# A fixed TensorE order for the small products of a chunked RWKV-7 scan, and two of its products interleaved

## The chip, the cores and the metric

The kernel runs on one core of a Trainium2 chip (trn2). The metric is the time of one execution on the device, in microseconds, of which the median over several runs is given. The core's engines work side by side, each through its own list of instructions: TensorE (PE in the profile, with its weight loads shown apart as PEld), VectorE (DVE), ScalarE (ACT), GpSimd (POOL) and SyncE (SP, which issues most transfers). They meet at semaphores.

## The reference

A decoder block of width 1024 over 1024 tokens. One projection feeds two groups of heads: a spatial gating unit and an RWKV-7 recurrence with 8 heads of 64. Their outputs go through `w_out`, then comes a cross attention over 256 memory tokens and a last RMS norm. All of it is in float32. The change touches the recurrence only:

```python
def rwkv7_step(state, inp):
    r, w, k, v, a, bb = inp
    sa = jnp.einsum('bhvk,bhk->bhv', state, a)
    state = state * w[:, :, None, :] + sa[..., None] * bb[:, :, None, :] + v[..., None] * k[:, :, None, :]
    y = jnp.einsum('bhvk,bhk->bhv', state, r)
    return state, y
...
_, y = lax.scan(rwkv7_step, state0, (r, decay, k, v, -kk, kk * icl))
```

## The kernel before

The large projections run as triples of matmuls (`mm3`, lines 177 to 179): every operand is split into a high and a low part, and three products of 128 x 128 by 128 x 512 are summed. They are called dense steps below.

The recurrence is cut into chunks of 64 tokens. Work goes by halves of a head pair: 4 pairs of heads, 2 halves of 512 tokens, so 8 units `u` of 8 chunks, and a unit has two quarters of 4 chunks. The two heads of a pair (`hh`) lie on partitions 0 to 63 and 64 to 127 (`R[0]`, `R[1]`). A unit goes through these steps, all of them small float32 products:

- `grams(i)` (lines 639 to 684): for each quarter 16 products of 64 x 64 by 64 x 128 (line 655). A product reads head `hh` from one half of the partitions and writes to half `x`, so the 16 use all four 64 x 64 quarters of the array (row half `hh`, column half `x`). The results lie in two PSUM banks, one for each head. From them VectorE makes masked matrices, which go to DRAM (`nt_scr`) and come back as diagonal blocks of 16 x 16. VectorE inverts these in a loop (lines 672 to 678) and the result returns through DRAM (`t_img`) as `t16`, in four transfers (line 683).
- `turn(n)` (lines 687 to 704) transposes operands on TensorE.
- `solve(i)` (lines 706 to 751) builds the inverse of a 64 x 64 triangular matrix for each chunk and head out of `t16`. It is a chain of stages. Each is a `pair_mm` (lines 713 to 718): 16 products of 64 x 64 by 64 x 64, eight chunks by two heads, on two quarters of the array, rows and columns `R[hh]`. The four on the chain write to the bank `cb`; VectorE works on the result (lines 731, 734 and 735, 739, 743) before the next may start. The last two, `at` by `tt` to `cb` and `tt` by `akv` to `co`, have no VectorE step between them. ScalarE copies their results to `ra` (line 747) and, in four pieces, to `avt` (line 750).
- `serial(i)` (lines 753 to 790) carries the state over the chunks, with two products for each (lines 773 and 780) and VectorE between them.
- `outputs(n)` (lines 792 to 803): 8 products of 128 x 64 by 64 columns for each quarter (line 800). `finish(u)` follows.

`drive` (lines 897 to 922) puts these steps and the dense steps into one order, by estimated costs and due times. A second scheduler, the one of the language, then sets the order on each engine when the kernel is built, and it may move instructions past each other. So the order on TensorE isn't the one of the code. `cb_ps` has one buffer, `co_ps` two.

Of the kernel before, what the change touches and what calls it, by code (L numbers as in the profile page):

```python
# [18 lines left out]
P = 128  # L19
# [4 lines left out]
NC = HT // C  # L24
# [4 lines left out]
QC = 4  # L29
# [53 lines left out]
def tile_hybrid_block(ctx: ExitStack, tc: tile.TileContext, x, xT, mem, memT, cst_d, vec_d, w_sv, w_blk, w2_d, a2_d,  # L83
# [372 lines left out]
    with tc.tile_pool(name="rw", bufs=1) as rw:  # L456
# [182 lines left out]
        def grams(i):  # L639
# [6 lines left out]
            for j in range(2):  # L646
                gr = rw.tile([P, QC, 2, C], F32, name="gr", bufs=4)
                an = rw.tile([P, QC, C], F32, name="an", bufs=2)
                nt1 = rw.tile([P, QC, C], F32, name="nt1", bufs=2)
                ak1 = rw.tile([P, QC, C], F32, name="ak1", bufs=2)  # L650
                pss = [co_ps().rearrange("p (c x t) -> p c x t", c=QC, x=2) for _ in range(2)]
                for c in range(QC):
                    cc = QC * j + c
                    for hh, x in ((0, 0), (1, 1), (0, 1), (1, 0)):
                        nc.tensor.matmul(pss[hh][R[x], c, :, :], bk[R[hh], cc, x, :], ra[R[hh], cc, :, :],  # L655
                                         start=True, stop=True)
                for hh in (1, 0):
                    ps = pss[hh]
                    if hh == 0:
                        nc.vector.tensor_tensor(out=an, in0=ps[:, :, 1, :], in1=m_a, op=ALU.mult)  # L660
                    else:
                        nc.vector.tensor_tensor(out=nt1[64:128], in0=ps[0:64, :, 1, :], in1=m_a[0:64], op=ALU.mult)
                        nc.vector.tensor_tensor(out=ak1[64:128], in0=ps[64:128, :, 1, :], in1=m_a[64:128], op=ALU.mult)
                    nc.sync.dma_start(out=ns[j, hh, :, 0:C, :].rearrange("c s t -> s c t"), in_=(an, nt1)[hh][R[hh]])
                    nc.vector.tensor_tensor(out=gr[:, :, hh, :], in0=ps[:, :, 0, :], in1=m_r, op=ALU.mult)
                    yield
                quarters[2 * i + j].update(gr=gr, ntl=(an, nt1), akl=(an, ak1))
                if j == 0:

                    L, X = [flat(t)[0:64].rearrange("p (s t) -> p s t", s=16) for t in (ak1, nt1)]  # L670
# [16 lines left out]
        def turn(n):  # L687
# [15 lines left out]
            q.update(avt=avt, bkt=bkt)  # L703
            yield

        def solve(i):


# [3 lines left out]

            def pair_mm(ps, fl, fr):
                ps = ps.rearrange("p (c t) -> p c t", c=NC)
                for c in range(NC):
                    for hh in range(2):
                        nc.tensor.matmul(ps[R[hh], c, :], fl(hh, c), fr(hh, c), start=True, stop=True)  # L717
                return ps

            tt = rw.tile([P, NC, C], F32, name="tt")  # L720
# [21 lines left out]
            ps = pair_mm(cb_ps(), lambda hh, c: z2[R[hh], c, :], lambda hh, c: tt[R[hh], c, :])  # L742
            nc.vector.tensor_tensor(out=tt[:, :, 32:64], in0=tt[:, :, 32:64], in1=ps[:, :, 32:64], op=ALU.add)
            yield
            ps = pair_mm(cb_ps(), lambda hh, c: at[R[hh], c, :], lambda hh, c: tt[R[hh], c, :])
            pa = pair_mm(co_ps(), lambda hh, c: tt[R[hh], c, :], lambda hh, c: akv[R[hh], c, :])
            nc.scalar.copy(out=ra[:, :, 1, :], in_=ps)
            for j in range(2):
                for hh in range(2):
                    nc.scalar.copy(out=qs[j]["avt"][R[0], :, R[hh]], in_=pa[R[hh], QC * j:QC * j + QC, :])  # L750
            yield

        def serial(i):
# [38 lines left out]
        def outputs(n):  # L792
# [1 line left out]
            q, u = quarters[n], quarters[n]["u"]  # L794
            gr, avt = q["gr"], q["avt"]
            yps = psC.tile([P, 512], F32, name="yps")
            for c in range(QC):
                for hh in range(2):
                    o = P * (c // 2) + 64 * hh
                    nc.tensor.matmul(yps[R[c % 2], o:o + 64], gr[:, c, hh, :], avt[:, c, R[hh]], start=True, stop=True)  # L800
            yt = u["y"][:, 2 * (n % 2):2 * (n % 2) + 2, :]
            nc.vector.tensor_tensor(out=yt, in0=yt, in1=yps[:, 0:256].rearrange("p (c v) -> p c v", c=2), op=ALU.add)
            yield
# [400 lines left out]
```

## Time and profile before

| | |
|---|---|
| runs shown | 953.72, 956.23 and 956.41 us, median 956.23 us |
| the profiled execution | 960.05 us, its span 958.3 us |
| PE busy | 926.8 us, 97% of the span |
| DVE busy | 582.0 us, 61% |
| ACT busy | 396.3 us, 41% |
| mean granted TensorE clock | 0.990 |

The span runs from the first to the last instruction. The busy time of an engine is the union of its instructions; where matmuls overlap, it counts once. A float32 product is two records in the profile (two passes), one of a dense step is one.

### The profile page before, as it was taken

The page shows a single profiled execution, that of the slowest core. Times are in us where ns is not written, and L with a number is a line of the kernel's source. Part 1 is how long each engine was busy: PE and PEld are TensorE (multiplying, and loading weights), DVE is VectorE, ACT ScalarE, POOL GpSimd, SP SyncE. Part 2 cuts the span into 40 slices and gives each one's busy share as a digit, 9 for nine tenths or more (in the row PEclk, how much of TensorE's full clock was granted, in tenths as well). Part 3 has the DMA queues.
Part 4 walks back from the last instruction along what each step waited for, and adds up shares of the span by engine and source line. Part 5 has one row for each costly group of instructions (what it writes and reads, how often), then busy time and mean ns, then how long its engine had stood idle before and what let it go on. Part 6 is the DMA issues. An engine that isn't in the chain of part 4 may idle for free.

```text
span 958.3 us, 17336 instructions
## 1 busy us (share of the span) xinstructions
PE 926.8 (97%) x6876; PEld 747.4 (78%) x6876; DVE 582.0 (61%) x1307; ACT 396.3 (41%) x802; POOL 49.6 (5%) x113
## 2 busy tenths in 40 slices
PE   6999999999999999999999999999899999999997
PEld 6978888888777777777777776777698778888885
DVE  5867233344674958586858698787677664433333
ACT  6753222225352526162526372435256653333222
POOL 0001000011000000000000000000000000000000
PEclk9999999999999999999999999899999999999999
DMA  9762011223121111111111174324462400000011
GB/s 318 256 213 80 31 66 66 68 72 109 36 58 36 40 23 50 35 51 30 52 32 43 27 211 148 101 60 141 150 211 70 123 22 1 23 23 23 28 39 44
DMA packets 86096, 76.93 MB, mean 80 GB/s; under 512 B 38272, under 2 KB 58752, under 8 KB 86016
## 3 DMA queue, kind: packets, MB, share of 16 engines
q1 hardware_dynamic: 84864, 73.73, 25.3%
q10 hardware_dynamic: 1152, 2.10, 0.6%
q8 instruction: 54, 0.88, 0.4%
q14 instruction: 26, 0.21, 0.1%
HBM read 62.17 MB, written 13.64 MB: 79 GB/s over the span
## 4 chain that ended last, share of the span: by engine, by line
PE 80%; DVE 8%; DMA 5%; ACT 3%; issue 3%; POOL 1%; POOLq 0%; SPq 0%; ACTq 0%; DVEq 0%
PE mm L177 21%; PE mm L179 20%; PE mm L178 20%; PE cb L717 4%; PE co L655 3%; PE co L717 2%; PE us L773 2%; PE us L780 1%; DMA w_raw<-y_scr 1%; PE yps L800 1%; POOL grs L153 1%; DMA w_raw<-in_w_sv 1%; DMA p_raw<-in_w_kv 1%; PE co L634 1%; PE co L432 1%
## 5 line engine op out<-in xcount | busy, mean ns | idle before, releaser
L177 PE MATMUL mm<-xh,w_hi 128*128 128x512 f32 x400 | 166.1, 415 | 0.0
L178 PE MATMUL mm<-xl,w_hi 128*128 128x512 f32 x400 | 160.0, 400 | 0.0
L179 PE MATMUL mm<-xh,w_lo 128*128 128x512 f32 x400 | 159.4, 398 | 0.0
L157 DVE TENSOR_TENSOR w_lo<-w_raw,w_hi 128x512 fp32r<-128x512 f32 x115 | 78.6, 686 | 62.0 <-ACT w_hi L156 61.3
L156 ACT CAST w_hi<-w_raw 128x512 fp32r<-128x512 f32 x115 | 70.9, 617 | 103.7 <-PE mm L178 90.6
L179 PEld LDWEIGHTS mm<-xh,w_lo 128*128 128x128 f32 x400 | 75.2, 188 | 15.6 <-issue 0.9
L177 PEld LDWEIGHTS mm<-xh,w_hi 128*128 128x128 f32 x400 | 75.3, 188 | 15.3 <-issue 2.1
L178 PEld LDWEIGHTS mm<-xl,w_hi 128*128 128x128 f32 x400 | 75.4, 188 | 14.2 <-issue 1.3
L177 PE MATMUL mm<-wo,w_hi 128*128 128x512 f32 x128 | 53.9, 421 | 0.0
L179 PE MATMUL mm<-wo,w_lo 128*128 128x512 f32 x128 | 53.0, 414 | 0.0
L178 PE MATMUL mm<-wo,w_hi 128*128 128x512 f32 x128 | 52.4, 409 | 0.0
L177 PE MATMUL mm<-vp_h,p_hi 128*128 128x512 f32 x128 | 51.3, 401 | 0.0
L498 ACT ACTIVATE t<-mm,vec 128x512 f32<-128x512 f32 x34 | 23.3, 687 | 65.0 <-PE mm L179 52.8
L179 PE MATMUL mm<-kp_h,w_lo 128*128 128x512 f32 x128 | 50.1, 391 | 0.0
L177 PE MATMUL mm<-kp_h,w_hi 128*128 128x512 f32 x128 | 50.0, 391 | 0.0
L179 PE MATMUL mm<-vp_h,p_lo 128*128 128x512 f32 x128 | 50.0, 390 | 0.0
L178 PE MATMUL mm<-vp_l,p_hi 128*128 128x512 f32 x128 | 49.9, 390 | 0.0
L178 PE MATMUL mm<-kp_l,w_hi 128*128 128x512 f32 x128 | 49.9, 389 | 0.0
L1041 DVE TENSOR_REDUCE mx<-mm 128x2 f32<-128x512 f32 x16 | 11.1, 691 | 41.8 <-PE mm L179 41.8
L655 PE MATMUL co<-ra,bk 64*64 64x128 f32 x512 | 35.5, 282 | 0.5 <-ACT avt L750 0.2
L786 DVE SCALAR_TENSOR_TENSOR stdiag<-us,dc,sd 64x64 f32<-64x64 f32 x112 | 31.7, 283 | 4.4 <-PE us L780 0.7
L789 ACT COPY ytok<-us 64x128 f32<-64x128 f32 x60 | 15.4, 256 | 43.6 <-DVE stdiag L786 34.1
(276 smaller groups left out, 2035.9 us busy)
## 6 DMA issues: line engine op xcount, KB each, us to landing
w_raw<-in_w_blk SPq DMA_DIRECT2D x50, 256.0 KB, 2.8
w_raw<-y_scr SPq DMA_DIRECT2D x32, 256.0 KB, 3.6
w_raw<-in_w_kv SPq DMA_DIRECT2D x17, 256.0 KB, 3.9
xr<-in_xT SPq DMA_DIRECT2D x8, 512.0 KB, 5.3
w_raw<-in_w_out SPq DMA_DIRECT2D x16, 256.0 KB, 2.8
h_all<-in_x SPq DMA_DIRECT2D x16, 256.0 KB, 5.0
pr<-in_w_qT SPq DMA_DIRECT2D x8, 512.0 KB, 4.5
w_raw<-in_w_o SPq DMA_DIRECT2D x16, 256.0 KB, 2.7
```

The lines of the kernel that those rows point to most:

```text
L156: nc.scalar.copy(out=hi, in_=src)
L157: (eng or nc.vector).tensor_tensor(out=lo, in0=src, in1=hi.bitcast(F32), op=ALU.subtract)
L177: nc.tensor.matmul(ps, lh, rh, start=first, stop=False)
L178: nc.tensor.matmul(ps, lh, rl, start=False, stop=False)
L179: nc.tensor.matmul(ps, ll, rh, start=False, stop=last)
L498: nc.scalar.activation(out=t1[:, 1:HT + 1], in_=ps, func=AF.Copy, scale=vc("mu", b))
L655: nc.tensor.matmul(pss[hh][R[x], c, :, :], bk[R[hh], cc, x, :], ra[R[hh], cc, :, :], start=True, stop=True)
L717: nc.tensor.matmul(ps[R[hh], c, :], fl(hh, c), fr(hh, c), start=True, stop=True)
L773: nc.tensor.matmul(us[:, 0, :], ra[:, c, :, :], s_old, start=True, stop=True)
L786: nc.vector.scalar_tensor_tensor(out=s_new[h2, h2], in0=us[h2, 1, h2], scalar=dcc[h2], in1=sd[h2, h2], op0=ALU.mult, op1=ALU.add)
L789: nc.scalar.copy(out=yc, in_=us[R[0], 0, :])
L1041: nc.vector.tensor_reduce(out=m2, in_=ps.rearrange("p (h m) -> p h m", h=2), axis=AX.X, op=ALU.max)
```

## The change

Three places get a block `with together():`, in which TensorE keeps the order of the code: the 16 products of `grams` (line 655), every `pair_mm` and the 8 products of `outputs`. In `pair_mm` and `outputs` that order now runs from the last chunk to the first, and in `pair_mm` from head 1 to head 0. The last two stages of `solve` become one loop of 32 products. For each chunk there are two to `cb` on the quarters (row half, column half) = (0, 0) and (1, 1), as before, and two to `co` on (0, 1) and (1, 0): their results change halves, and the ScalarE copies read the other half.

```diff
--- before.py
+++ after.py
@@ -649,11 +649,11 @@
                 nt1 = rw.tile([P, QC, C], F32, name="nt1", bufs=2)
                 ak1 = rw.tile([P, QC, C], F32, name="ak1", bufs=2)
                 pss = [co_ps().rearrange("p (c x t) -> p c x t", c=QC, x=2) for _ in range(2)]
-                for c in range(QC):
-                    cc = QC * j + c
-                    for hh, x in ((0, 0), (1, 1), (0, 1), (1, 0)):
-                        nc.tensor.matmul(pss[hh][R[x], c, :, :], bk[R[hh], cc, x, :], ra[R[hh], cc, :, :],
-                                         start=True, stop=True)
+                with together():
+                    for c in range(QC * j, QC * j + QC):
+                        for hh, x in ((0, 0), (1, 1), (0, 1), (1, 0)):
+                            nc.tensor.matmul(pss[hh][R[x], c % QC, :, :], bk[R[hh], c, x, :], ra[R[hh], c, :, :],
+                                             start=True, stop=True)
                 for hh in (1, 0):
                     ps = pss[hh]
                     if hh == 0:
@@ -703,6 +703,10 @@
             q.update(avt=avt, bkt=bkt)
             yield
 
+        def together():
+
+            return tc.manual_schedule(engines={mybir.EngineType.PE})
+
         def solve(i):
 
 
@@ -712,9 +716,10 @@
 
             def pair_mm(ps, fl, fr):
                 ps = ps.rearrange("p (c t) -> p c t", c=NC)
-                for c in range(NC):
-                    for hh in range(2):
-                        nc.tensor.matmul(ps[R[hh], c, :], fl(hh, c), fr(hh, c), start=True, stop=True)
+                with together():
+                    for c in range(NC - 1, -1, -1):
+                        for hh in (1, 0):
+                            nc.tensor.matmul(ps[R[hh], c, :], fl(hh, c), fr(hh, c), start=True, stop=True)
                 return ps
 
             tt = rw.tile([P, NC, C], F32, name="tt")
@@ -742,12 +747,18 @@
             ps = pair_mm(cb_ps(), lambda hh, c: z2[R[hh], c, :], lambda hh, c: tt[R[hh], c, :])
             nc.vector.tensor_tensor(out=tt[:, :, 32:64], in0=tt[:, :, 32:64], in1=ps[:, :, 32:64], op=ALU.add)
             yield
-            ps = pair_mm(cb_ps(), lambda hh, c: at[R[hh], c, :], lambda hh, c: tt[R[hh], c, :])
-            pa = pair_mm(co_ps(), lambda hh, c: tt[R[hh], c, :], lambda hh, c: akv[R[hh], c, :])
+
+            ps, pa = [t.rearrange("p (c t) -> p c t", c=NC) for t in (cb_ps(), co_ps())]
+            with together():
+                for c in range(NC - 1, -1, -1):
+                    for r in R:
+                        nc.tensor.matmul(ps[r, c, :], at[r, c, :], tt[r, c, :], start=True, stop=True)
+                    for hh in range(2):
+                        nc.tensor.matmul(pa[R[1 - hh], c, :], tt[R[hh], c, :], akv[R[hh], c, :], start=True, stop=True)
             nc.scalar.copy(out=ra[:, :, 1, :], in_=ps)
             for j in range(2):
                 for hh in range(2):
-                    nc.scalar.copy(out=qs[j]["avt"][R[0], :, R[hh]], in_=pa[R[hh], QC * j:QC * j + QC, :])
+                    nc.scalar.copy(out=qs[j]["avt"][R[0], :, R[hh]], in_=pa[R[1 - hh], QC * j:QC * j + QC, :])
             yield
 
         def serial(i):
@@ -794,10 +805,12 @@
             q, u = quarters[n], quarters[n]["u"]
             gr, avt = q["gr"], q["avt"]
             yps = psC.tile([P, 512], F32, name="yps")
-            for c in range(QC):
-                for hh in range(2):
-                    o = P * (c // 2) + 64 * hh
-                    nc.tensor.matmul(yps[R[c % 2], o:o + 64], gr[:, c, hh, :], avt[:, c, R[hh]], start=True, stop=True)
+            with together():
+                for c in range(QC - 1, -1, -1):
+                    for hh in range(2):
+                        o = P * (c // 2) + 64 * hh
+                        nc.tensor.matmul(yps[R[c % 2], o:o + 64], gr[:, c, hh, :], avt[:, c, R[hh]],
+                                         start=True, stop=True)
             yt = u["y"][:, 2 * (n % 2):2 * (n % 2) + 2, :]
             nc.vector.tensor_tensor(out=yt, in0=yt, in1=yps[:, 0:256].rearrange("p (c v) -> p c v", c=2), op=ALU.add)
             yield
```

What it makes of TensorE's order is shown at three places. The first is the end of a solve and the grams behind it, in the fourth unit whose solve is followed by both. `tt,at` and `akv,tt` are the last two stages, `us` the state's products, `xh`, `xl` with `w_hi`, `w_lo` dense steps. Before:

```order
L717 MATMUL cb<-tt,at 64x64 x16
L717 MATMUL co<-akv,tt 64x64 x16
L773 MATMUL us<-stdiag_1924,ra 128x128
L655 MATMUL co<-ra,bk 64x128 x8
L780 MATMUL us<-avt,bkt 128x128
L655 MATMUL co<-ra,bk 64x128 x8
L179 MATMUL mm<-xh_99,w_lo 128x512
L773 MATMUL us<-stdiag_1925,ra 128x128
L655 MATMUL co<-ra,bk 64x128 x8
L177 MATMUL mm<-xh_100,w_hi 128x512
L655 MATMUL co<-ra,bk 64x128 x8
L780 MATMUL us<-avt,bkt 128x128
```

Now:

```order
L755 MATMUL cb<-tt,at 64x64 x2
L757 MATMUL co<-akv,tt 64x64 x2
L655 MATMUL co<-ra,bk 64x128
L179 MATMUL mm<-xh_100,w_lo 128x512
L177 MATMUL mm<-xh_101,w_hi 128x512
L784 MATMUL us<-stdiag_1924,ra 128x128
L178 MATMUL mm<-xl_109,w_hi 128x512
L179 MATMUL mm<-xh_101,w_lo 128x512
L177 MATMUL mm<-xh_102,w_hi 128x512
L791 MATMUL us<-avt,bkt 128x128
L655 MATMUL co<-ra,bk 64x128 x15
L784 MATMUL us<-stdiag_1925,ra 128x128
```

Before, the 16 products of a quarter stood in two groups of 8, one for each head, with other work between, and the two stages stood one behind the other. Now the 16 are 1 and 15 (so in all 16 quarters, and the one stands directly behind a solve's last product for 7 of them), and the two stages alternate by twos; the first seven such pairs of rows are left out ahead of the fence.

The second place is the solve's first stage of the same unit, which waits for `t16` (here `t_`, with `an` or `nt` as the other operand). Before, its second half:

```order
L177 MATMUL mm<-xh_102,w_hi 128x512
L717 MATMUL cb<-t_4122,an 64x64
L178 MATMUL mm<-xl_110,w_hi 128x512
L179 MATMUL mm<-xh_102,w_lo 128x512
L177 MATMUL mm<-xh_103,w_hi 128x512
L717 MATMUL cb<-t_4122,nt_4040 64x64
L717 MATMUL cb<-t_4122,an 64x64
L717 MATMUL cb<-t_4122,nt_4040 64x64
L717 MATMUL cb<-t_4122,an 64x64
L717 MATMUL cb<-t_4122,nt_4040 64x64
L717 MATMUL cb<-t_4122,an 64x64
L717 MATMUL cb<-t_4122,nt_4040 64x64
```

Now its end and what follows:

```order
L722 MATMUL cb<-t_4221,nt_4101 64x64
L722 MATMUL cb<-t_4221,an 64x64
L722 MATMUL cb<-t_4221,nt_4101 64x64
L722 MATMUL cb<-t_4221,an 64x64
L179 MATMUL mm<-xh_103,w_lo 128x512
L177 MATMUL mm<-xh_104,w_hi 128x512
L178 MATMUL mm<-xl_112,w_hi 128x512
L179 MATMUL mm<-xh_104,w_lo 128x512
L177 MATMUL mm<-xh_105,w_hi 128x512
L178 MATMUL mm<-xl_113,w_hi 128x512
L722 MATMUL cb<-zz_1926,tt 64x64 x16
```

Before, the 16 products stood as 1, 7, 1 and 7 with dense steps between, in each of the 8 solves. Now they follow each other without a break, the last chunk first.

The third place is the last solve of the program. Before, from the end of its third stage:

```order
L717 MATMUL cb<-t_6558,an 64x64
L717 MATMUL cb<-t_6558,nt_6481 64x64
L177 MATMUL mm<-wo,w_hi 128x512
L178 MATMUL mm<-wo,w_hi 128x512
L179 MATMUL mm<-wo,w_lo 128x512
L177 MATMUL mm<-wo,w_hi 128x512
L717 MATMUL cb<-tt,zz_1927 64x64 x16
L178 MATMUL mm<-wo,w_hi 128x512
L179 MATMUL mm<-wo,w_lo 128x512
L177 MATMUL mm<-wo,w_hi 128x512
L717 MATMUL cb<-tt,at 64x64 x16
L717 MATMUL co<-akv,tt 64x64 x16
```

Now, likewise:

```order
L722 MATMUL cb<-t_6789,nt_6674 64x64
L722 MATMUL cb<-t_6789,an 64x64
L722 MATMUL cb<-tt,zz_1927 64x64 x16
L755 MATMUL cb<-tt,at 64x64 x2
L757 MATMUL co<-akv,tt 64x64 x2
```

The dense steps between the stages are gone there: all four stages and the last 32 products stand in a row (64 and 32 products), behind 29 dense steps and four transposes that stand ahead of the first. In the other solves at least one dense step, mostly three, still stands between two stages.

Counted over the whole program, stretches in which TensorE leaves the full 128 x 128 array for quarters or halves of it and comes back were 131 and are now 112. No product is added or taken away.

## Rows read from the trace of the kernel before

**Rows 1.** The page's busy times: us, share of the span, instructions.

```profile
PE 926.8 (97%) x6876; PEld 747.4 (78%) x6876; DVE 582.0 (61%) x1307; ACT 396.3 (41%) x802; POOL 49.6 (5%) x113
```

**Rows 2.** The page's busy tenths in 40 slices, TensorE and its granted clock.

```profile
PE   6999999999999999999999999999899999999997
...
PEclk9999999999999999999999999899999999999999
```

**Rows 3.** The page's chain that ended last, by engine.

```profile
PE 80%; DVE 8%; DMA 5%; ACT 3%; issue 3%; POOL 1%; POOLq 0%; SPq 0%; ACTq 0%; DVEq 0%
```

**Rows 4.** Timeline of PE, a piece of 7 products: start, length, instruction, count.

```profile
486.46 0.40 PE L177 MATMUL mm<-xh,w_hi 128*128 128x512 f32 x1
486.79 0.27 PE L717 MATMUL cb<-t,nt 64*64 64x64 f32 x1
...
487.39 0.50 PE L178 MATMUL mm<-xl,w_hi 128*128 128x512 f32 x1
487.73 0.39 PE L179 MATMUL mm<-xh,w_lo 128*128 128x512 f32 x1
487.96 0.40 PE L177 MATMUL mm<-xh,w_hi 128*128 128x512 f32 x1
```

**Rows 5.** Timeline of PE, grams of one quarter in two halves.

```profile
351.24 1.09 PE L655 MATMUL co<-ra,bk 64*64 64x128 f32 x16
352.26 0.49 PE L780 MATMUL us<-avt,bkt 128*128 128x128 f32 x2
352.68 1.09 PE L655 MATMUL co<-ra,bk 64*64 64x128 f32 x16
353.70 0.50 PE L178 MATMUL mm<-xl,w_hi 128*128 128x512 f32 x1
```

**Rows 6.** Timeline of PE, the first unit's second quarter, in one piece.

```profile
263.16 1.33 PE L655 MATMUL co<-ra,bk 64*64 64x128 f32 x32
264.42 0.50 PE L177 MATMUL mm<-xh,w_hi 128*128 128x512 f32 x1
```

**Rows 7.** Timeline of PE, the last two stages of the last solve.

```profile
648.34 1.15 PE L717 MATMUL cb<-tt,at 64*64 64x64 f32 x32
649.32 1.10 PE L717 MATMUL co<-akv,tt 64*64 64x64 f32 x32
650.35 0.49 PE L773 MATMUL us<-stdiag,ra 128*128 128x128 f32 x2
```

**Rows 8.** PE's waits: us in total, times, longest.

```profile
PE us L773 <- ACT ytok L789: 1.8, 4, 0.6
PE cb L717 <- DVE t L734: 1.5, 2, 1.0
PE us L780 <- DVE avt L774: 1.2, 2, 0.7
...
PE cb L717 <- DMA t<-t_img: 0.5, 1, 0.5
```

**Rows 9.** Timelines of PE and SP: a unit's last half of grams, and its `t16` transfers.

```profile
501.77 1.09 PE L655 MATMUL co<-ra,bk 64*64 64x128 f32 x16
...
530.46 2.57 SPq L683 DMA_DIRECT2D t<-t_img  x4
...
606.79 1.97 PE L655 MATMUL co<-ra,bk 64*64 64x128 f32 x16
...
633.17 3.27 SPq L683 DMA_DIRECT2D t<-t_img  x4
```

**Rows 10.** The tile `t`: the time from issue to landing of its transfers.

```profile
DMA to landing us min/median/max: 2.3/2.5/4.1
```

**Rows 11.** Timelines of DVE and ACT in the last solve: start, length, instruction, count, idle time.

```profile
647.55 0.42 DVE L743 TENSOR_TENSOR tt<-tt,cb 128x256 f32<-128x256 f32 x1 [0.86 <-PE cb L717]
...
649.53 0.58 ACT L747 COPY ra<-cb 128x512 f32<-128x512 f32 x1 [4.50 <-PE cb L717]
650.47 1.52 ACT L750 COPY avt<-co 64x256 f32<-64x256 f32 x4 [0.35 <-PE co L717]
```

**Rows 12.** Windows: busy us (instructions) of PE, PEld, DVE, ACT, POOL; granted clock, DMA share, GB/s.

```profile
500.00:550.00 50.00, 48.72 (x517) 37.58 (x519) 37.13 (x102) 22.38 (x48) 3.21 (x10) 1.00 0.15 36
604.00:608.00 4.00, 4.00 (x34) 3.09 (x34) 2.98 (x7) 0.78 (x1) 0.00 (x0) 0.61 0.37 104
608.00:612.00 4.00, 4.00 (x21) 3.18 (x17) 2.46 (x7) 0.73 (x2) 0.00 (x0) 0.53 0.11 23
```

## The prediction

> **What bounds the kernel.** I read the busy times first [rows 1]: TensorE is busy for 97% of the span. The reader is to see that it is the only candidate, though matmuls overlap, so that its busy share doesn't say how fast it works. The slices [rows 2] show that this holds nearly everywhere, the recurrence included, and the chain that ended last [rows 3] has 80% on PE. So what PE doesn't have to do is time won, as long as no wait takes its place. The waits [rows 8] are short: the largest of the recurrence add up to 1.8, 1.5, 1.2 and 0.5 us. The question is then what small products cost on PE, and the timelines tell it.
>
> A dense step takes 0.23 us (487.73 to 487.96 [rows 4]). The piece of 7 products between 486.46 and 487.73 takes 1.27 us with two dense steps, so 0.81 by itself. Its seven products lie on two quarters of the array, four on the fuller one. The last two stages of a solve take 0.98 and 1.03 us for 16 products each [rows 7], eight to a quarter, so 0.12 us for each product that a quarter does. Four are 0.47 us, and 0.34 us of the 0.81 are the way out of the full array and back. I use 0.34 us for each such excursion.
>
> Grams of 8 products on two quarters take 1.02 us from their start to the next instruction [rows 5]; with 0.1 us on the way in and 0.1 us for the slower dense step behind (both as in [rows 4]: 0.33 and 0.34 us instead of 0.23) that is 1.22 us. The reader should set against it the one quarter whose 16 products the scheduler had left mixed over all four array quarters [rows 6]: 1.26 us to the next instruction, for twice the products, and 2 x 1.02 for the halves. **Four quarters of the array work side by side; two halves behind each other waste half of it.**
>
> **The change, part by part.**
>
> *Grams.* Before: 24 halves by themselves (24 x 1.22 = 29.3 us), four directly behind a solve (4 x 0.87 = 3.5, the 1.22 less 0.34 us), two quarters in one piece (2 x 1.46 = 2.9, from [rows 6] with the 0.2 us). That is 35.7 us. Now 16 times 15 products, four on the fullest quarter, as many as in a half: 16 x 1.22 = 19.5 us. The 16 single ones cost 0.22 us of work (two of these products take a quarter of 0.87), nine of them with an excursion of their own: 9 x 0.56 + 7 x 0.22 = 6.6. Sum 26.1, saved 9.6 us. If all 15 ran as slowly as [rows 6], 0.24 us more each, it would be 5.8.
>
> *The last two stages.* Side by side on four quarters, eight products on each, they need the time of one stage. Each solve saves 2.01 - 1.03 = 0.98 us [rows 7], and eight solves 7.8 us. Taken as 7.5, since no row shows 64 columns on four quarters; the bounds are 0 and 7.8.
>
> *Pieces.* Eight first stages stood as 1, 7, 1 and 7: 2 x (0.46 + 0.81) = 2.54 us against 1.28 for one of 16 (0.94 + 0.34), so 10.1 us are saved. Taken back: 11 other stages now stand in two or three pieces, 12 excursions more, 4.1 us. Four excursions go in the last solve (1.4), two of the outputs (0.7), and two single pieces had stood inside output stretches already (-0.7). Sum 7.4 us.
>
> Together 9.6 + 7.5 + 7.4 = 24.5 us. The excursions counted over the whole order agree: 131 become 112, and 19 x 0.34 = 6.5 us of the sum are theirs. ScalarE and VectorE keep their instructions, transfers likewise, so there is no term for them; the copies that read another half of the bank are costed at nothing, since four such copies already move between halves or stay, two by two.
>
> **What is given back.** PE gets shorter, the chains beside it don't.
>
> *Waiting for `t16`.* From a unit's last grams to the last of the four transfers it takes a long loop on VectorE and two trips through DRAM. In the sixth unit the last half starts at 501.77, the four issues end at 533.03 and the last landing is some 2.5 us behind its issue [rows 9, 10]: about 34 us. In the last unit (606.79, 636.44) it is about 32. Before, the pieces of the first stage rode on the four landings, each with dense steps around it. Now the first product waits for the last landing, and all PE work between has to cover it. Counted in the order, at 0.23 us for each dense step, 0.22 for a state product and 1.28 or 0.34 as above, that work is now 31 to 34 us in the first five units, but 27 us in the sixth (52 dense steps instead of 75 up to the first piece), 32 in the seventh and 28 in the last. If every chain is as long as it was, PE waits some 7 us in the sixth, 4 in the seventh, 3 to 4 in the last and 1 elsewhere: 16 us. If VectorE gets to the loop earlier by what PE gains, nothing. I take 8, the middle; the other waits below overlap with it, and VectorE at 37 of 50 us [rows 12] isn't full.
>
> *The last solve.* Its four stages now follow each other bare. Each waits for the last product's record (0.27 us [rows 4]), a VectorE step of 0.42 us [rows 11], and the signals, about 0.1. I take 0.8 us four times, 3.2 us; the dense steps that had stood there run at another place and save nothing.
>
> *Behind a solve.* Both products now end together. The copy to `ra` (0.58) and four to `avt` (1.52 us [rows 11]) come after, where the first had lain beside the second stage. The 15 grams need the bank that these copies free, 2.3 us or so after; the order leaves 2.1 us of PE work. I take 0.3 us by 7, 2 us. The state's products stand closer to each other as well; their waits of 3 us [rows 8] may grow by 1.
>
> *Not lost again:* of PE's waits for these same things some 3 us [rows 8] are in the time already.
>
> So 8 + 3.2 + 2 + 1 - 3 = 11 us come back, and **24.5 - 11 = 13.5, taken as 14 us**. The profiled execution took 960.05 us, 3.8 above the median; the sum would make it 946, and the median 956.2 becomes **942 us**.
>
> The clock: PE was granted 0.61 and 0.53 of full speed in 604 to 612 [rows 12], the lower level of 1.2 GHz for most of it. Ahead of it stood the small products of a solve and of grams with almost no dense step. There the new order has dense steps between, but the bare last solve is a like stretch. I count one such fall for one, within 3 us either way.
>
> **The skill on the four quarters.** The trace has two row halves writing to one bank at full rate: both stages of [rows 7] do so, from rows 0 to 63 and 64 to 127. The Trainium skill's page "TensorEngine Tiling (Array Packing)" says, under "Gotcha 1: PSUM Pressure", that different row tiles can't access the same PSUM bank at the same time. By that rule the 32 products, in which each bank gets both row halves, would not run four abreast, and the time would be 949.5 us; but the two abreast of before couldn't either, and the trace decides against it.
>
> **The rivals.**
>
> 1. *No wait grows.* VectorE and the transfers follow PE, and all 24.5 us stay: 931.7 us. For it: VectorE has a quarter of its time free. Against: the 27 and 28 us above. Chance 0.17.
>
> 2. *Issue limits the 32 products.* They need 64 records in 0.98 us, 15 ns apiece; the densest rows have 32 in 1.26 and 32 in 0.98 us, 39 and 31 ns [rows 6, 7]. If PE can't start them closer than the latter, the 32 products take 2 us as before, the 7.5 us go, and the time is 949.5 us. Against: in both rows the quarters are the limit, not the issue, so the rate of issue is not shown. The Trainium skill's page "TensorE: Matmul & The Clock Gate", under "Wait — 56ns, not 53.3ns?", has a floor of about 25 ns from start to start however small the product; by that the 64 records would take 1.6 us, an estimate, and the time would be 946 us. No row here runs closer on the average, so the trace is open on it. Chance 0.10.
>
> 3. *The chain through `t16` sets the pace.* All eight units wait for the last landing; the gain is eaten by 21 to 27 us of waits, and the time is within 0.3% of before, 954 to 959 us. Against: five of eight units have 31 us or more of cover. Chance 0.07.
>
> 4. *Slower.* The same chain gets longer, because the grams of both heads now end together and their five masked products queue on VectorE while the transfers to `nt_scr` go out later. It decides from 3 us on: with 34 us made 37 in every unit the waits are 16 + 8 x 2 to 3, about 35 us, with the other 6 some 41 against 24.5, and less 3 that were there: 13 us slower, 970 us. Against: the old second half of the grams ended later than the new 15 do. Chance 0.05.
>
> **How the numbers follow.** The forecast, part of the gain kept, has 0.61: 934 to 950 us. With rival 1 (0.17), rival 2 (0.10), rival 3 (0.07) and rival 4 (0.05) that is all. Faster by over 0.3% (about what a measurement of this kernel can tell from no change) are the forecast and rivals 1 and 2: 0.88. Within 0.3%: 0.07. Slower: 0.05. The range takes in most of rival 1 and all of rival 2, with the bounds of the `t16` term on the forecast (0 to 16 us instead of 8, the half of it within reach on either side): 931 to 951 us.
>
> **What would show it.** In the new profile the grams stand as x30 at some 1.0 to 1.1 us, and the 64 records of a solve's end take about 1.0 us instead of 2.0: that is the mechanism. Waits before the first `cb` product of a solve, by a transfer, of 3 to 7 us in the sixth and last units, and waits of 0.8 us by lines 736 to 748 of VectorE in the last, show what is given back. The prediction is wrong if those 64 records take 1.6 us or more, if PE's waits between 260 and 680 us grow by over 20 us, or if they don't grow.

## The result, and the profile after

The changed kernel took **970.72 us** (median of 4 runs, 967.58 to 973.66) against 956.32 us for the kernel before on the same chip: ratio 1.0149, interval 1.0103 to 1.0194. Forecast were 942 us, 931 to 951. The profiled execution of the change took 967.58 us, 3.1 below its median, and that of before 960.05, 3.7 above; so the two traces lie 7.2 us apart (spans 965.5 and 958.3), the medians 14.4. What is read from the two traces below bears on the 7.2 us alone.

The page's busy times of the change, beside [rows 1]:

```profile
PE 907.2 (94%) x6876; PEld 726.6 (75%) x6876; DVE 579.8 (60%) x1307; ACT 397.0 (41%) x802; POOL 48.8 (5%) x113
```

PE is busy for 19.6 us less and the span is 7.2 us longer, so PE stood idle for 27 us more. The slices show where:

```profile
PE   6999999999999999999999798988699999999997
...
PEclk9999999999999999999999799999999999999999
```

Each slice is 24 us. Slices 23 to 29 (531 to 700 us) have five digits under 9; in [rows 2] it is one, an 8. The timeline of PE at a solve's end, with the grams behind it (start, length, instruction, count):

```profile
352.66 0.27 PE L755 MATMUL cb<-tt,at 64*64 64x64 f32 x2
...
353.60 0.23 PE L757 MATMUL co<-akv,tt 64*64 64x64 f32 x2
353.64 0.38 PE L655 MATMUL co<-ra,bk 64*64 64x128 f32 x2
353.95 0.50 PE L177 MATMUL mm<-xh,w_hi 128*128 128x512 f32 x1
...
356.04 1.10 PE L655 MATMUL co<-ra,bk 64*64 64x128 f32 x30
357.10 0.49 PE L784 MATMUL us<-stdiag,ra 128*128 128x128 f32 x2
```

The reader sees the mechanism at work: 64 records of the last two stages from 352.66 to 353.64, 0.98 us where [rows 7] have 2.01, and 15 grams in 1.06 us, where [rows 5] have 1.02 us for 8. PE's waits in the change (engine, line, releaser: total, times, longest), beside [rows 8]:

```profile
PE yps L837 <- DVE ytok L833: 16.2, 8, 5.5
PE mm L177 <- ACT w_hi L156: 9.1, 4, 6.4
PE mm L177 <- DMA w_raw<-y_scr: 7.7, 1, 7.7
PE us L784 <- ACT ytok L800: 3.2, 9, 1.5
PE cb L722 <- DVE zz L736: 2.0, 1, 2.0
...
PE cb L722 <- DMA t<-t_img: 1.1, 1, 1.1
...
PE cb L755 <- DVE tt L748: 0.5, 1, 0.5
PE cb L722 <- DVE t L739: 0.5, 1, 0.5
PE cb L722 <- DVE zz L744: 0.5, 1, 0.5
```

In the trace of before, the lines for the same two places, `finish` and the first step behind the last unit (`ktt` by `p_hi`; its wait is put down to no releaser):

```profile
PE mm L177 <- issue: 2.6, 1, 2.6
PE yps L824 <- DVE ytok L820: 1.0, 1, 1.0
```

The largest, 16.2 us, is at a line that the change doesn't touch: the four transposes of `finish`, once in each unit. They wait for VectorE's last scaling (line 833), which follows POOL's power (line 153). The wait for `w_hi` is at the program's start and old. The wait for `t16`, to which the forecast gave 8 us, is 1.1.

**Three places.** The first is `finish`. The chain from a unit's last outputs, timelines of VectorE, of before and then of the change, with PE's transposes:

```profile
343.55 0.69 DVE L820 TENSOR_TENSOR ytok<-ytok,grs 128x512 f32<-128x512 f32 x1 [1.76 <-POOL grs L153]
...
358.75 0.49 PE L824 MATMUL yps<-cst,ytok 128*128 128x128 f32 x3
```

```profile
341.51 0.69 DVE L833 TENSOR_TENSOR ytok<-ytok,grs 128x512 f32<-128x512 f32 x1 [1.76 <-POOL grs L153]
...
342.35 0.63 PE L837 MATMUL yps<-cst,ytok 128*128 128x128 f32 x4 [1.40 <-DVE ytok L833]
```

Before, the transposes came 14 us after the scaled `ytok`; now they stand right behind it and PE waits. Counted in the order, at the durations of the prediction, 22 to 24 us of PE work stood between a unit's last outputs and these transposes in the first five units; now it is 8, 8, 8, 7.5 and 4.7.

The second place is the sixth unit's stretch. Timeline of PE in the change:

```profile
535.86 0.40 PE L179 MATMUL mm<-xh,w_lo 128*128 128x512 f32 x1
541.77 1.09 PE L837 MATMUL yps<-cst,ytok 128*128 128x128 f32 x4 [5.51 <-DVE ytok L833]
543.94 0.37 PE L722 MATMUL cb<-t,nt 64*64 64x64 f32 x1 [1.09 <-DMA t<-t_img]
...
546.29 0.79 PE L177 MATMUL mm<-wo,w_hi 128*128 128x512 f32 x1 [0.38 <-ACT w_hi L156]
```

The row at 535.86 is the last dense step on `xh`; the next dense step, the first of `w_out`, starts at 546.29. For 10 us there is none to fill a wait. Why, the windows tell: instructions of line 178 alone, one for every third dense step, from the first grams of the first unit to those of the sixth, and from there to the last `finish` (us of PE, PEld, clock, DMA share, GB/s). Before, then the change:

```profile
259.10:497.00 237.90, 64.86 (x158) 29.85 (x158) 1.00 0.16 41
497.00:679.80 182.80, 52.37 (x128) 24.35 (x128) 0.98 0.36 101
```

```profile
258.40:503.20 244.80, 71.85 (x177) 33.35 (x177) 1.00 0.17 43
503.20:688.00 184.80, 48.53 (x117) 22.34 (x117) 0.95 0.34 96
```

In the first five units the change does 19 times three dense steps more, 57 x 0.23 = 13 us, so they last longer though their own products take less. These steps come from the last three units and the end. The last three take 184.8 us with 33 dense steps fewer. Their mean granted clock is 0.95 for 0.98. The stretches at the lower of its two levels (0.50), before and then in the change (columns as in [rows 12]):

```profile
604.90:611.70 6.80, 6.80 (x40) 5.21 (x37) 4.72 (x12) 1.51 (x3) 0.00 (x0) 0.50 0.18 37
```

```profile
539.00:552.70 13.70, 9.47 (x93) 7.20 (x95) 7.98 (x15) 4.92 (x8) 1.83 (x2) 0.50 0.75 211
651.70:655.10 3.40, 2.88 (x56) 2.69 (x52) 0.65 (x2) 0.62 (x1) 0.00 (x0) 0.50 0.73 216
```

In them PE was busy for 6.8 us before and for 12.4 now, so the clock costs some 3 us of PE's time there (an estimate: half of the difference).

The third place is the end. After the last `finish` 4 dense steps are left where there were 28, while its result goes through DRAM: 7.7 us of wait for `y_scr`, where PE stood idle for 2.6 us at the same step before.

Sum, of 27 us more idle time: `finish` 16.2 - 1.0 = 15 (5.5 of it in the sixth unit's stretch); the end 7.7 - 2.6 = 5; the last solve's bare stages 3.6 (the rows of lines 736 to 748); some 3 in many small waits.

### The profile page after: what moved, and what is told of

It reads as the page before. It is cut to its first block, busy times and chain, and to the rows that moved or that the text cites. A ratio compares the mean times of both kernels' runs of the same rounds, so it can differ in the third digit from the quotient of the medians.

```text
span 965.5 us, 17337 instructions
## 1 busy us (share of the span) xinstructions
PE 907.2 (94%) x6876; PEld 726.6 (75%) x6876; DVE 579.8 (60%) x1307; ACT 397.0 (41%) x802; POOL 48.8 (5%) x113
## 4 chain that ended last, share of the span: by engine, by line
PE 78%; DVE 7%; DMA 6%; ACT 4%; issue 3%; POOL 1%; SPq 1%; POOLq 0%; DVEq 0%; ACTq 0%
PE mm L177 20%; PE mm L179 20%; PE mm L178 20%; PE cb L722 4%; PE us L784 2%; PE co L722 2%; PE co L655 2%; PE us L791 2%; POOL grs L153 1%; DMA xr<-in_xT 1%; DMA w_raw<-y_scr 1%; PE yps L812 1%; DMA w_raw<-in_w_o 1%; DMA w_raw<-in_w_sv 1%; DVE w_lo L157 1%
## 5 line engine op out<-in xcount | busy, mean ns | idle before, releaser
L177 PE MATMUL mm<-xh,w_hi 128*128 128x512 f32 x400 | 162.1, 405 | 0.0
L179 PE MATMUL mm<-xh,w_lo 128*128 128x512 f32 x400 | 161.7, 404 | 0.0
L784 PEld LDWEIGHTS us<-stdiag,ra 128*128 128x128 f32 x120 | 18.6, 188 | 18.1 <-ACT ytok L800 14.4
L784 PE MATMUL us<-stdiag,ra 128*128 128x128 f32 x120 | 27.7, 313 | 3.6 <-ACT ytok L800 3.2
```

The costliest lines, as they stand in the source:

```text
L177: nc.tensor.matmul(ps, lh, rh, start=first, stop=False)
L179: nc.tensor.matmul(ps, ll, rh, start=False, stop=last)
L784: nc.tensor.matmul(us[:, 0, :], ra[:, c, :, :], s_old, start=True, stop=True)
```

## The experiments

Four theories stand in the texts on record. **A**: the waits at `finish` are the loss. **B**: the stages that now stand together in a solve cost it. **D**: the blocks make the language's scheduler pull dense steps and `finish` forward, until dense steps run out in the sixth unit. **C**: a loop from a unit's grams through VectorE, `t16` and the solve sets a pace that PE has outrun. Each ratio is to runs of the kernel before on the same chip. Times of before lay between 952 and 962 us, medians 955.9 to 956.6.

**1. Without the block around the grams** (the other edits stay):

```diff
-                with together():
-                    for c in range(QC * j, QC * j + QC):
+                for c in range(QC):
```

> The change without its block around the grams; the other three edits stay. Theory A (the block around the grams makes the scheduler put the four transposes of finish some 8 us of PE work behind a unit's last outputs instead of some 20, so PE waits there for the chain through POOL's power; the saving on PE itself is real): here 19, 19, 20, 19, 13 and 16 us of PE work stand there again in the first six units, so waits for line ytok at the transposes fall from 16.2 to under 4 us, the clock fall at 539 to 553 us goes, PE stays busy for some 907 us, the wait for y_scr near the end stays at 7 to 8 us (4 dense steps of cover as in the change), and the time is 936 to 945 us. Theory B (the stages of the solve that now stand together are what costs: late t16, bare stages, copies that end late): nothing of that is undone here, the time stays at 960 us or more.

Measured: 953.57 us, ratio 0.9979 (0.9959 to 1.0). PE busy 906.5 us. Its waits:

```profile
PE mm L177 <- ACT p_hi L156: 7.7, 1, 7.7
PE cb L722 <- DVE zz L736: 4.0, 5, 1.1
PE yps L837 <- DVE ytok L833: 3.4, 3, 1.6
```

One block of the three carries the loss: 17 us come back, and B falls. The waits at `finish` went as A said, and the end stayed (7.7 us, at the same step). But the time missed A's 936 to 945 us: PE is busy for 20 us less than before and the medians differ by 2.6. PE's idle time in the traces is 45 us instead of 31: 5 us of the growth are the end, 4 the waits for `zz`, 2 `finish`, the rest small.

**2. The block around the grams alone**, on the kernel before.

> The block around the grams alone, on the kernel before. Counted in the order PE has 8 us more to do than before (167 excursions instead of 131). Theory A: the finish transposes stand 12, 9, 10.5, 9, 7, 7.5, 7 and 6 us of PE work behind the last outputs, so waits for ytok there of 8 to 16 us, and the wait for y_scr near the end is 7 to 8 us instead of 2.6 (3 dense steps of cover); with the 8 us of excursions the time is 975 to 990 us. Theory B: none of the solve's edits is here, so the time is that of before plus the 8 us at most, 956 to 965 us.

Measured: 984.89 us, ratio 1.03 (1.0251 to 1.0349); waits at `finish` 6.6 us in 7, at the end 8.0, for `t16` 3.5. The profiled executions lie 23 us apart: 7 of them are PE work (busy 934.0), 14 the growth of these three waits. The time lies in A's range and not in B's; the waits at `finish` are fewer than A's 8 to 16 us.

**3. The last two stages alone**, on the kernel before (one loop of 32 products, as in the change).

> The last two stages of a solve as one loop of 32 products on four quarters alone, with its block, on the kernel before. Counted in the order PE has 15 us less to do than before (8 us by the quarters, 7 by single products and pieces that go). Theory A: the finish transposes stand 21, 21, 22, 20, 21, 13, 11 and 6 us behind the last outputs and 28 dense steps cover the end as before, so waits grow by 3 us at most: 940 to 946 us, with the 64 records in 0.95 us. Theory B: the copies behind the 32 products end late and the state waits, so PE's waits grow by 8 us or more and the time is 950 to 957 us.

Measured: 952.61 us, ratio 0.9957 (0.9933 to 0.9981). PE busy 916.1, 10.7 us less than before; waits for the state's copies (`ytok`) 4.7 us instead of 1.8. Faster, but by 3.5 us, not A's 10 to 16. The time lies in B's range, but B's reason isn't there: PE's idle time grew by 3.5 us, not by 8 or more. So neither theory says what takes the rest.

**4. `finish` later** in the planner's order for the first six units, the whole change else:

```diff
-                    (ok(n - 1), lambda: finish(halves_u[n - 1]), D_F, W_F, 0)) if on]
+                    (ok(n - 1), lambda: finish(halves_u[n - 1]), D_F, (W_F if n >= 7 else (0.35, 0.6)), 0)) if on]
```

> The whole change, with finish put later in the planner's order (its share of the stretch 0.35 to 0.6 instead of 0.08 to 0.36) for all units but the last. The PE work is that of the change. The transposes of finish now stand 26, 20, 15, 7, 10, 10, 4 and 5 us of PE work behind the last outputs (8, 8, 8, 7.5, 5, 6, 7 and 6 in the change). Theory A: in the first, second, third, fifth and sixth unit the waits for ytok go, 1.4 + 1.6 + 1.3 + 5.5 + 1.6 = 11.4 us, and the clock fall at 539 to 553 us with them, some 7 us; the last two wait 3 to 4 us longer; the end stays uncovered: 954 to 962 us. Theory B: the solve's stages are unchanged, 966 to 974 us.

Measured: 964.43 us, ratio 1.0078 (1.0049 to 1.0106). The time lies between A's range and B's. The waits at `finish` fell from 16.2 to 6.8 us, and the time by 6.3 only. The timeline of PE in the sixth unit's stretch says why:

```profile
530.05 0.40 PE L179 MATMUL mm<-xh,w_lo 128*128 128x512 f32 x1
...
540.23 0.80 PE L177 MATMUL mm<-wo,w_hi 128*128 128x512 f32 x1 [6.77 <-ACT w_hi L156]
```

The same hole of 10 us stands there with `finish` out of the way: it belongs to the dense steps, whose next weights aren't there, and without `finish` PE waits for those. This part is D's.

**5. The whole order held**: the block put around all of the recurrence, so that PE's order is the planner's; the inner blocks go.

```diff
-        with nullcontext():
+        with tc.manual_schedule(engines={mybir.EngineType.PE}):
             for n in range(-2, NH):
```

> The whole change, with TensorE's order held not in single stages but over all of the recurrence, as the planner drive writes it. Counted in the order PE has 17 us less to do than in the change (73 excursions instead of 112), no dense step is pulled ahead (96 for each of the first units, in the change 102 to 109) and 12 us of PE work stand between a unit's last outputs and the transposes of finish, 4 in the last. Theory D (the loss of the change is that the language's scheduler, seeing the blocks, pulls dense steps and the transposes of finish forward, so that the sixth unit runs out of dense steps before the weights of w_out are there; from 535.9 to 546.3 us no dense step runs in the change): the waits of finish go but for the last unit's 4 to 6 us, no stretch without dense steps in the sixth unit, and the time is 925 to 942 us. Theory B (the stages that stand together in a solve cost the time themselves): they stand together here as well, 955 us or more.

Measured: 981.98 us, ratio 1.0265 (1.0235 to 1.0296). D's numbers failed; B's number (955 us or more) held, but this run can't tell B from another cause of waits. PE busy is down to 901.3 us, and the waits are others:

```profile
PE cb L722 <- DMA t<-t_img: 18.4, 7, 6.7
PE co L655 <- DVE gr L665: 16.7, 15, 2.3
```

Here PE waits most for `t16` and for VectorE between the two quarters of grams.

**6. Without POOL's power**, the whole change else.

```diff
-            rsqrt_small(rs, sv, 1.0 / C, 64e-5, rw)
+            nc.vector.tensor_scalar(out=rs, in0=sv, scalar1=0.0, scalar2=0.1, op0=ALU.mult, op1=ALU.add)
```

> The whole change, with the power on POOL in finish left out (its result is a constant that still depends on the sum, from one step on VectorE), so the chain to the transposes of finish is 2 to 3 us shorter; the output is not normalized. The order is nearly that of the change (8, 8, 8, 7.5, 5, 8, 5.5 and 7 us of PE work behind the last outputs). Theory A (the finish waits themselves are the loss): the seven waits of 1.3 to 1.7 us go, the one of 5.5 us falls to some 3, the clock fall there gets shorter: 950 to 957 us. Theory D (dense steps run out in the sixth unit): the small waits go, but in the sixth unit the wait for the landing of t (1.1 us before) and for the first step of w_out grows by what finish no longer takes: 959 to 964 us.

Measured: 955.84 us, ratio 0.9997 (0.9974 to 1.002). A was right on the size, D too high: some 2 us off this chain are worth 15 us over eight units (the two traces, 954.0 and 965.5 us long, show 11.5 of them, all idle time of PE). The dense steps stand as far forward as in the change, line 178 with x177 in the first five units and x117 behind:

```profile
259.30:497.70 238.40, 71.98 (x177) 33.36 (x177) 1.00 0.17 44
497.70:676.40 178.70, 49.42 (x117) 22.57 (x117) 0.96 0.35 99
```

So their place alone doesn't cost the 15 us: the first five units are as long as before with the 13 us of dense steps more. In the sixth unit the hole stays, with two waits in it:

```profile
534.57 0.63 PE L837 MATMUL yps<-cst,ytok 128*128 128x128 f32 x4 [3.79 <-DVE ytok L833]
537.84 0.37 PE L722 MATMUL cb<-t,nt 64*64 64x64 f32 x1 [2.63 <-DMA t<-t_img]
```

**7. `finish` early in the kernel before**: `W_F`, the share of a unit's stretch in which the planner puts `finish`, is `(0.0, 0.1)` instead of `(0.08, 0.36)`.

> The kernel before, with finish put at the start of the planner's stretch (0 to 0.1 instead of 0.08 to 0.36), nothing else. 8, 7, 8, 7, 9, 11, 10 and 6 us of PE work then stand behind the last outputs, in the first units as in the change; PE has 3.6 us less to do (124 excursions), dense steps are not pulled ahead and 28 of them cover the end as before. Theory A: waits for ytok of 1.4 to 3 us in the first five units, some 9 us more than before, and 958 to 964 us. Theory D: the waits are the same, but PE makes up for them where they only move work, so 952 to 960 us, and no stretch without dense steps in the sixth unit.

Measured: 954.61 us, ratio 0.9983 (0.9953 to 1.0013). A missed: waits at `finish` are 3.5 us in 6 where it wanted 10. D's range holds the time, though it wanted the same waits. Transposes near their operand cost nothing by themselves. What the change has besides is a longer chain on VectorE. From the sum of a unit's last outputs to the scaled `ytok`, second unit, in the change and then in this run:

```profile
384.23 0.42 DVE L815 TENSOR_TENSOR ytok<-ytok,yps 128x256 f32<-128x256 f32 x1
...
391.66 0.69 DVE L833 TENSOR_TENSOR ytok<-ytok,grs 128x512 f32<-128x512 f32 x1 [1.75 <-POOL grs L153]
```

```profile
386.48 0.42 DVE L802 TENSOR_TENSOR ytok<-ytok,yps 128x256 f32<-128x256 f32 x1 [0.89 <-PE yps L800]
...
392.22 0.69 DVE L820 TENSOR_TENSOR ytok<-ytok,grs 128x512 f32<-128x512 f32 x1 [1.75 <-POOL grs L153]
```

That is 7.4 us against 5.7: in the change seven other instructions of VectorE stand between the steps of `finish` (3.5 us in all), here two (1.1 us). Over the first five units the time from PE's last output to the scaled `ytok` is 8.8 to 9.9 us in the change and 6.1 to 8.5 here, with 4.5 to 8 us of PE work beside it there and 6 to 8 here. So the near place costs only where the chain is longer than PE's work beside it.

**8. The kernel before, its whole order held** (the edit of 5).

> The kernel before, its order on TensorE held over all of the recurrence as the planner writes it; none of the change's own edits. Counted in the order PE has 34 us less to do than before and 7.5 us more than the held change, the two stages behind each other instead of side by side. Theory D: the time is that of the held change and 5 to 8 us on top, 932 to 948 us. Theory C (a loop from a unit's grams through VectorE, t16 and the solve to the next grams sets some 46 to 47 us for each unit, whatever PE has to do): as long as the held change within 3 us.

Measured: 981.14 us, ratio 1.0273 (1.0223 to 1.0322): as long as 5, though PE has 7.5 us more to do by the order. That is what C said: in a held order, what the change saves on PE is worth nothing.

**9 and 10. A shorter loop** on VectorE, in the change and in the kernel before:

```diff
-            for s in range(1, 15):
+            for s in range(1, 8):
```

> The whole change, with VectorE's loop that inverts the diagonal blocks cut from 14 passes to 7 (the inverse is left incomplete), so the chain from a unit's grams to t16 is some 9 to 10 us shorter. The scheduler's order then keeps 96 dense steps in each of the first units, finish has 11 to 16 us of PE work ahead of it, 21 dense steps cover the end, and PE has 8 us less to do by the order. Theory C (what takes the gain is that PE has outrun the unit's loop from the grams through VectorE and t16 to the solve; the scheduler fills the time with dense steps from later and with finish, and these are then missing): without that loop the gain of the change shows, 920 to 930 us, and 3 to 8 us less than the same cut of the kernel before. Theory B (the stages that stand together cost the time): the change stays behind the same cut of the kernel before by 10 us or more.

> The same cut of VectorE's loop from 14 passes to 7 in the kernel before (the inverse is left incomplete). By the order PE has 28 us less to do than before (83 excursions instead of 131). If PE alone sets the time, as the prediction took it, 956 - 28 and a few us of waits: 928 to 934 us. Theory C: the same, since PE is the limit of the kernel before as long as the loop is covered. Theory B has no view on it.

Measured: 935.31 us, ratio 0.9779 (0.9754 to 0.9803), and 943.15, ratio 0.9858 (0.9836 to 0.9881). Both are some 5 to 10 us above what was expected, but **now the change is 7.8 us faster than its counterpart**, where it was 14.4 slower with the full loop. C said 3 to 8 us, and B's 10 us behind fall. The windows over line 178, of the first five units, of 9 and then of 10:

```profile
257.80:477.40 219.60, 60.74 (x152) 28.79 (x152) 1.00 0.17 44
```

```profile
257.80:483.90 226.10, 60.56 (x152) 28.81 (x152) 1.00 0.17 43
```

With the same number of dense steps in both, the five units are 6.5 us shorter. The scheduler's order changed with the loop, so the two runs show loop and order together, and C isn't shown by them alone.

**11. A combination that might beat both**: the last two stages as one loop with its block, the block in `outputs`, none elsewhere, `W_F = (0, 0.3)`.

> The part of the change that paid (the last two stages on four quarters) with the block in outputs, no block in grams or in the other stages, and finish put earlier in the planner's stretch (0 to 0.3). By the order PE has 20 us less to do than before and 5 us less than the last two stages alone; 9 to 16 us of PE work stand ahead of the transposes of finish, 96 dense steps in the first units, 25 cover the end. If a gain on PE shows where finish, the dense steps and the end stay covered: 945 to 951 us. If the waits take it again as in the runs so far: 952 to 955 us.

Measured: 952.38 us, ratio 0.997 (0.995 to 0.9991). The second case: PE is busy for 911.9 us, 15 less than before, and 3.5 us are gained.

**12. The block split by bank**, the whole change else:

```diff
-                with together():
-                    for c in range(QC * j, QC * j + QC):
-                        for hh, x in ((0, 0), (1, 1), (0, 1), (1, 0)):
+                for hh in (1, 0):
+                    with together():
+                        for c in range(QC * j, QC * j + QC):
+                            for x in range(2):
```

> The whole change, with the block of the 16 grams split into two of 8, one for each bank, as the kernel before had them; each is still held in order. PE's work by the order is that of the change. Theory D (a block that needs both banks at once is what makes the scheduler pull finish and dense steps forward): finish has 19, 19, 20, 19, 13 and 16 us ahead of it, 96 dense steps stand in each of the first units and 12 cover the end, so waits for ytok at the transposes are 2 to 4 us in all, no stretch without dense steps in the sixth unit, and the time is 948 to 954 us, as without the block. Theory B: as long as the change, 966 us or more.

Measured: 954.36 us, ratio 0.9966 (0.9945 to 0.9987). As D said, if 0.4 us above its range: 16 us come back, line 178 stands x162 in the first five units (158 before, 177 in the change), and the waits at `finish` are down:

```profile
PE mm L177 <- DMA w_raw<-y_scr: 5.2, 1, 5.2
...
PE yps L838 <- DVE ytok L834: 3.5, 3, 1.7
```

So a held order of the grams doesn't move the rest; the one block over both banks does, in which the products of the two heads are mixed. This run parts the block and the heads at once, and no run has one block with the heads in turn, so which of the two counts isn't separated.

## Why the prediction was wrong

*The gain on PE was nearly right.* 24.5 us were forecast. Busy time fell by 19.6, and the lower clock of the last three units hides some 3 more (the estimate above). Grams of 15 took 1.06 us, the 64 records 0.98. Rival 2, and with it the 39 and 31 ns of [rows 6, 7] as a limit, is out.

*The failed step is "What is given back".* It priced the waits of the chains whose products the diff names, and not what the new order did to the others. It took 11 us to come back; 27 us did. The four transposes of `finish` had 14 us to spare before in the first five units, and the prediction never looked where they now stood, nor at the chain on VectorE that they wait for: 15 us. The dense steps were counted (52 instead of 75 in the sixth unit), but set against `t16` (1.1 us measured for 8) and not followed to where they had gone, which was forward, so that the sixth unit and the end were bare: 5 us at the end, and a hole of 10 us with a clock fall in it. The window of that stretch (columns as in [rows 12]):

```profile
536.30:546.20 9.90, 3.06 (x36) 2.50 (x36) 6.73 (x12) 3.17 (x5) 2.27 (x3) 0.64 0.75 215
```

PE was idle for some 7 of these 10 us, and 0.64 is a mean of its two levels. "One fall for one" was wrong for this reason: 6.8 us at the lower level became 17.1.

*What the sum doesn't hold.* The forecast missed by 28.7 us. The two traces show 21 of them: 16 us of waits, 5 of busy time. The other 7 lie between the traces and the medians, and no trace shows them; the mean granted clock of before is 0.990 in its profiled execution and 0.995 in the median of its runs beside the experiments, that of the change 0.982 to 0.985. And run 1, without the block around the grams, still took 953.6 us where 942 were forecast: some 12 us of the miss are there without that block, and their cause stays open.

*Right in the small:* the last solve gave back 3.6 us for 3.2, but as one wait of 2.0 and three of 0.5 where four of 0.8 were counted, so the sum is luck; the state's waits for `ytok` grew from 1.8 to 3.2 us for the 1 forecast.

*The rivals.* Rival 4 has the time (970 us) but not the mechanism. Its chain through `t16` is a large wait only under a held order (run 5), so the number is luck. Rival 1 would need waits that follow PE; they don't: in runs 1, 3, 11 and 12 PE is busy for 11 to 20 us less than in the trace of before (up to 4 us of that belong to the long execution that was profiled) and the time is 1.6 to 3.6 us less. The sign "PE's waits between 260 and 680 us grow by over 20 us" came out on its edge: PE is busy there for 409.9 us before and 390.0 now.

*What is shown, and what isn't.* Shown: the loss hangs on the block over both banks with the heads mixed in it (1, 2, 12); the chain of `finish` carries some 15 us of it (6), by its length and its place together, not by the place alone (7); the hole of dense steps is there without `finish` (4); with VectorE's loop shorter, and the order that goes with it, the change pays (9, 10). Open: why the scheduler answers such a block by pulling other work forward; what takes most of PE's gain in runs 1, 3, 11 and 12; and what holds the last three units at 176 to 187 us in all these runs but 2 and the held ones, with the loop shorter as well (179.3 and 179.9 us in 9 and 10).

## What to carry to other kernels

A busy share of 97% on an engine that has filler to move may say only that there is filler: before a saving on it is counted in full, find the loop that runs beside it and how much shorter than the engine's work it is. When a block or a new order is put on some instructions, compare the place of *all* others in the old and the new order, above all of those whose operands come off another engine, and count the filler that is left for each stretch up to the end. And, as run 12 suggests, hold a block to what one resource (here one PSUM bank) releases at once.

## What the runs showed of the hardware

Four quarters of the array ran 64 records in 0.94 us from first start to last (352.66 to 353.60), 15 ns apiece, with both row halves writing to each bank. The Trainium skill's page "TensorE: Matmul & The Clock Gate", under "Wait — 56ns, not 53.3ns?", has a floor of about 25 ns from start to start. The Trainium skill's page "TensorEngine Tiling (Array Packing)", under "Gotcha 1: PSUM Pressure", says that different row tiles can't access the same bank at the same time. Neither held for these products, and the measurement decides.

POOL's power on a tile of 128 x 8 took 1.64 us, ten times VectorE's scaling of the same tile (timelines of before):

```profile
341.63 0.16 DVE L152 TENSOR_SCALAR rs_t<-gsv 128x8 f32<-128x8 f32 x1
...
341.87 1.64 POOL L153 TENSOR_TENSOR grs<-rs_t,mhalf 128x8 f32<-128x8 f32 x1 [6.37 <-DVE rs_t L152]
```
